# Linear attention beside a delta-rule loop: the query transfers move from SP's queue to GpSimd's

## The chip, the cores and the metric

The kernel runs on one core of a Trainium2 chip. Its time is the device time of one launch in microseconds (us), as the median of several runs. Besides the timed runs one execution was recorded by the hardware profiler; all rows below come from that one. PE is the matrix engine (TensorE; PEld its weight loads), DVE is VectorE, ACT is ScalarE, POOL is GpSimd, and SP is SyncE, which here does nothing but issue DMA transfers. ACT and POOL issue some transfers too. Every engine works through its own instruction list strictly in order: an instruction that waits holds back all that stand behind it on that engine.

## The reference

One layer of a hybrid backbone over 1024 latent tokens and 256 context tokens of width 1024. What is computed, cut to the parts that matter here:

```
h  = modulate(x, norm1_g, sh1, sc1);  hc = modulate(ctx, ...)
zl = h @ w_in;  zc = hc @ w_in                  # three groups of heads
hy  = hyena_mix(zl_hy, ...)                      # long convolutions
gla = gla_branch(zl_gla, zc_gla, ...)            # linear attention, both directions
gdn = gdn_branch(zl_gdn, zc_gdn, ...)            # gated delta rule, both directions
x = x + g1 * (concat([hy, gla, gdn]) @ w_out)
x = x + g2 * (square(relu(modulate(x, norm2_g, ...) @ w1)) @ w2)
out = rmsnorm(x, final_norm_g)

# linear attention, per chunk of 64 tokens
attn = einsum(q, k, exp(b_i - b_j))              # b: running sum of the log gates
o    = (q * exp(b)) @ S + attn @ v
S    = exp(b_last) * S + (k * exp(b_last - b))^T v
```

The delta rule has the same shape of recurrence, one state per head and direction, with a triangular solve inside each chunk.

## The kernel before

The kernel is written with a tile framework that puts the instructions of each engine into one fixed order when the program is built. It works from a timeline of its own, in which each instruction has a priority from its place in the source and a modelled duration; semaphores between the engines are derived from the tiles. So an edit to one line can change the order on every engine.

Stages in time: the Hyena filters, the norm and the input projection; the Hyena convolutions; the preparation and triangular inverses of the delta rule; then, from about 695 to 900 us of the profile, linear attention and the delta-rule loop side by side; then the output projection (`w_out`, line 1706) and the MLP, both as seven-product matrix multiplications in three-pass fp32r (`stage`, line 1518).

Linear attention (`gla_pair`, line 760) works on two pairs of heads, pair 0 and then pair 1. The two heads of a pair lie on partitions 0 to 63 and 64 to 127. For six sizes s = 32 to 1 (levels 0 to 5) DVE and POOL form differences of the running sums, ACT takes their exponential, and DVE multiplies by the queries (line 792) and keys (line 799). The queries `eq` must then lie in a block-diagonal tile `bd`, so that one matmul serves both heads without mixing them: `place` (line 778) copies each half of 64 partitions with a DMA of 256 KB into its own block (line 781). Two `bd` tiles alternate. PE multiplies them with the keys (`pss<-bd,lv`, for the last ones `pss<-bd,kT`), and masked copies collect the result in `A`. Level 6 (the diagonal) is written into `bd` by ACT and has no transfer. Later in the pair, `place` is called once per direction for `q2` (line 882), which PE multiplies with the states `S` (`pss<-S,bd`, line 887). That makes 8 calls a pair, 16 calls and 32 transfers in all. The sources of the transfers are `lv` tiles, four of which rotate; one is free again when its transfer has landed. The pair ends with a norm, transposes (`pss<-ident,A` and `pss<-ident,vt`, line 913), a gate, and stores of its output to DRAM (`dy<-lv`, line 916).

The delta-rule loop (`gdn_head`, line 1122) has ten steps, 0 to 9, for four heads that run abreast. In each step PE multiplies the state with keys and queries (`psl<-S,kq`), solves (`psl<-r,NT`), updates the state (`psl<-vn,kv`) and forms outputs (`psl<-vn,at`). SP loads `at` and `kq` for each step (lines 1135 and 1142), two tiles of each per head; ACT loads `kv`.

After both, `load_y` (line 1343) reads the mixer's outputs back from DRAM into the tiles `h` (`h<-dy`, line 1350; the gates of the delta rule are `h<-dz_dg`, line 1094). These lie in memory that linear attention used. The first products of `w_out` need them, the weights `wr` (from SP, line 1502, and with accumulation from POOL, line 1496), and both split into a high and a low part: ACT casts (`S<-wr`, `T<-h`, line 292), POOL or DVE subtracts (line 252).

Of the kernel before, what the change touches and what calls it, by code (L numbers as in the profile page):

```python
# [17 lines left out]
L = 1024  # L18
# [193 lines left out]
class Build:  # L212
# [547 lines left out]
    def gla_pair(self, p, mid, G):  # L760

        nc = self.nc
# [15 lines left out]
        def place(bd, t):  # L778

            for hh, r in enumerate(halves):  # L780
                nc.sync.dma_start(bd[r, hh].rearrange("p n i -> p (n i)"), t[r, :L])
        for li, s in enumerate((32, 16, 8, 4, 2, 1, 0)):
            bd = self.bd[li % 2]
            if s:
                eq = self.lvt()
                v = lambda t: t[:, :L].rearrange("p (a h s) -> p a h s", h=2, s=s)
                nb = L // (2 * s)
                fm, rm = v(bf)[:, :, 0, s - 1:s], v(rb)[:, :, 1, 0:1]
                self.tt(v(eq)[:, :, 0, :], v(rb)[:, :, 0, :], rm.broadcast_to([128, nb, s]), SUB, self.eng("eqf", 7 * p + li))
                self.tt(v(eq)[:, :, 1, :], v(bf)[:, :, 1, :], fm.broadcast_to([128, nb, s]), SUB, self.eng("eqr", 7 * p + li))  # L790
                self.act(eq[:, :L], eq[:, :L], AF.Exp, scale=1.0 / 16)
                self.tt(eq[:, :L], eq[:, :L], qT, MUL, self.eng("qh0", 7 * p + li))
                place(bd, eq)
                if s > 1:
                    ek = self.lvt()
                    self.tt(v(ek)[:, :, 0, :], fm.broadcast_to([128, nb, s]), v(bf)[:, :, 0, :], SUB, self.eng("ekf", 7 * p + li))
                    self.tt(v(ek)[:, :, 1, :], rm.broadcast_to([128, nb, s]), v(rb)[:, :, 1, :], SUB, self.eng("ekr", 7 * p + li))
                    self.act(ek[:, :L], ek[:, :L], AF.Exp, scale=1.0 / 16)
                    self.tt(ek[:, :L], ek[:, :L], kT[:, :L], MUL, self.eng("kk", 7 * p + li))
                keys = ek if s > 1 else kT  # L800
            else:

                for hh, r in enumerate(halves):
                    self.twice(f"qd{hh}", p, bd[r, hh], c64(qT)[r, :, :])

            ps = self.pss.tile([128, 512], F32, name="pss").rearrange("p (h t i) -> p h t i", h=2, i=32)
            for n in range(16):
                for b in range(2):
                    c = 32 * (b if li else 1 - b)
                    r = 64 * (n % 2) + 32 * b  # L810
# [28 lines left out]
        for s0 in (0, 10):  # L839
            for d in range(2):  # L840
# [3 lines left out]
                for i, n in enumerate(ch):  # L844
                    r = slice(64 * (n % 2), 64 * (n % 2) + 64)
# [22 lines left out]
        for par in range(2):  # L868
            for b in range(2):
                r = slice(64 * par + 32 * b, 64 * par + 32 * b + 32)  # L870
# [7 lines left out]
        for d in range(2):  # L878
            e, q2 = self.lvt(), self.bd[1 - d]
            self.act(e[:, :L], cum[d][:, :L], AF.Exp, scale=1.0 / 16)  # L880
            self.tt(e[:, :L], e[:, :L], qT, MUL)
            place(q2, e)
            for t in range(8):
                for hh in range(2):
                    for par, r in enumerate(halves):
                        n = 2 * t + par
                        self.mm(ps[t // 2][r, t % 2, 96 * hh:96 * hh + 96], q2[:, hh, n, :], S[d][:, n, :], False, d == 1 and hh == 1 and t % 2 == 1)
# [920 lines left out]
```

## Time and profile before

| | us |
|---|---|
| median of 3 runs | 1639.69 (1637.02 to 1644.93) |
| profiled execution | 1637.75 |
| its span, first to last instruction | 1636.0 |
| PE busy | 1507.8 (92%) |
| DVE busy | 1211.8 (74%) |
| ACT busy | 803.2 (49%) |
| POOL busy | 642.4 (39%) |

The shares are averages over stages with different limits. In the stretch in which the change lies, 700 to 880 us, PE is busy for 143.19 of 180 us and POOL for 48.15. DMA-issuing instructions don't count as busy; where they are an engine's own work they are in the timeline of that engine.

### The profile page before, as it was taken

How to read it: one execution, taken by the hardware profiler on the slowest of the kernel's cores; microseconds unless marked ns; L12 is line 12 of the kernel's file. 1: busy time of each engine (PE TensorE's matmuls, PEld its weight loads, DVE VectorE, ACT ScalarE, POOL GpSimd, SP SyncE). 2: the span in 40 equal slices, each digit the busy share in tenths (PEclk: the TensorE clock that was granted, in tenths of full speed). 3: DMA queues.
4: the chain of work that ended last, by engine and by line, in shares of the span. 5: the costliest groups of instructions: out<-in, count | busy, mean ns of one | idle time of the engine just before them, and what ended most of it. 6: DMA issues, size and time to landing. Idle time of an engine off the chain costs nothing. (4 is left out here: it accounts for less than half of the span.)

```text
span 1636.0 us, 26277 instructions
## 1 busy us (share of the span) xinstructions
PE 1507.8 (92%) x10160; PEld 1216.2 (74%) x10160; DVE 1211.8 (74%) x1827; ACT 803.2 (49%) x1462; POOL 642.4 (39%) x478
## 2 busy tenths in 40 slices
PE   7799999989999898768879799999999999999996
PEld 2378877767688676657779587788888888888886
DVE  5963589897575487676678878987679758974995
ACT  5432222315655644454556356554565456446554
POOL 0311141331434330131243254655556555655554
PEclk9999999999999997778889899999999999999998
DMA  8432777756566531267657934364455535453532
GB/s 296 135 110 91 259 256 263 238 180 210 165 205 197 165 134 46 75 192 209 182 148 226 309 103 104 103 155 129 104 132 124 149 87 153 103 136 96 135 72 103
DMA packets 116852, 256.81 MB, mean 157 GB/s; under 512 B 29431, under 2 KB 74919, under 8 KB 103800
## 3 DMA queue, kind: packets, MB, share of 16 engines
q1 hardware_dynamic: 88360, 175.42, 32.4%
q0 software_dynamic: 9808, 59.77, 16.4%
q10 hardware_dynamic: 18560, 19.94, 4.0%
q8 instruction: 80, 1.31, 0.3%
q14 instruction: 44, 0.36, 0.1%
HBM read 196.57 MB, written 41.75 MB: 146 GB/s over the span
## 5 line engine op out<-in xcount | busy, mean ns | idle before, releaser
L224 PE MATMUL psb<-T,S 128*128 128x512 f32 (+1 forms) x3072 | 693.3, 387 | 9.7 <-ACT T L292 6.0
L224 PEld LDWEIGHTS psb<-T,S 128*128 128x128 f32 x3072 | 571.0, 188 | 130.9 <-ACT T L292 6.8
L252 POOL TENSOR_TENSOR S<-wr,S 128x512 fp32r<-128x512 f32 x252 | 365.4, 1465 | 303.2 <-ACT S L292 302.6
L292 ACT CAST S<-wr 128x512 fp32r<-128x512 f32 x252 | 155.1, 620 | 150.0 <-PE psb L224 104.6
L224 PE MATMUL psb<-ahi,wh 128*128 128x512 f32 x448 | 184.5, 413 | 9.3 <-DVE acc L260 4.8
L224 PE MATMUL psb<-alo,wh 128*128 128x512 f32 x448 | 182.8, 408 | 0.0
L224 PE MATMUL psb<-ahi,wl 128*128 128x512 f32 x448 | 181.6, 405 | 0.0
L252 POOL TENSOR_TENSOR wl<-ws,wh 128x1024 fp32r<-128x1024 f32 x28 | 71.1, 2538 | 209.7 <-ACT wh L292 139.1
L260 DVE SCALAR_TENSOR_TENSOR acc<-psb,vecs,acc 128x504 f32<-128x504 f32 (+5 forms) x168 | 111.3, 678 | 49.8 <-ACT acc L264 47.5
L260 DVE SCALAR_TENSOR_TENSOR x<-psb,modT,x 128x512 f32<-128x512 f32 (+1 forms) x148 | 105.2, 727 | 40.2 <-PE psb L224 39.9
L252 DVE TENSOR_TENSOR T<-h,T 128x512 fp32r<-128x512 f32 x88 | 85.8, 1004 | 48.8 <-ACT T L292 47.3
L224 PEld LDWEIGHTS psb<-ahi,wh 128*128 128x128 f32 x448 | 87.8, 196 | 40.7 <-issue 9.1
L252 DVE TENSOR_TENSOR T<-ar,T 128x512 fp32r<-128x512 f32 x112 | 111.0, 1018 | 6.1 <-ACT T L292 5.9
L224 PEld LDWEIGHTS psb<-alo,wh 128*128 128x128 f32 x448 | 87.7, 196 | 26.1 <-issue 8.2
L224 PEld LDWEIGHTS psb<-ahi,wl 128*128 128x128 f32 x448 | 87.6, 196 | 22.5 <-issue 5.1
L292 ACT CAST T<-ar 128x512 fp32r<-128x512 f32 x112 | 68.5, 620 | 44.7 <-DVE ar L260 27.8
L252 POOL TENSOR_TENSOR lv<-cum 128x512 f32<-128x512 f32 x21 | 31.3, 1510 | 83.2 <-PE pss L224 36.9
L264 ACT ACTIVATE acc<-psb,vecs 128x512 f32<-128x512 f32 (+1 forms) x48 | 31.1, 663 | 64.1 <-PE psb L224 31.4
L292 ACT CAST T<-h 128x512 fp32r<-128x512 f32 x88 | 52.6, 619 | 19.5 <-DMA h<-dy 10.4
L264 ACT ACT_TABLE_LOAD x27 | 34.6, 1283 | 35.4 <-DVE acc L260 16.3
L1779 ACT COPY ar<-psb 128x512 f32<-128x512 f32 x48 | 28.2, 587 | 48.2 <-PE psb L224 47.6
L292 ACT CAST wh<-ws 128x1024 fp32r<-128x1024 f32 x28 | 29.3, 1045 | 44.8 <-PE psb L224 35.5
(332 smaller groups left out, 2597.7 us busy)
## 6 DMA issues: line engine op xcount, KB each, us to landing
wr<-in_w SPq DMA_DIRECT2D x40, 1024.0 KB, 4.8
wr<-in_w POOLq DMA_DIRECT2D x24, 1024.0 KB, 8.0
mw<-in_wmod SPq DMA_DIRECT2D x32, 512.0 KB, 5.1
ws<-in_win SPq DMA_DIRECT2D x28, 512.0 KB, 4.1
dft<-in_fw POOLq DMA_DIRECT2D x8, 1024.0 KB, 6.0
dft<-in_iv POOLq DMA_DIRECT2D x8, 1024.0 KB, 6.6
bd<-lv SPq DMA_DIRECT2D x32, 256.0 KB, 4.0
wr<-wr POOLq DMA_DIRECT2D x8, 1024.0 KB, 7.2
```

Of the source, the lines that this page charges most:

```text
L224: return self.nc.tensor.matmul(out, lhsT=lhsT, rhs=rhs, start=start, stop=stop, skip_group_check=more)
L252: return (eng or self.nc.vector).tensor_tensor(out, a, b, op)
L260: return (eng or self.nc.vector).scalar_tensor_tensor(out, a, s, b, op0=op0, op1=op1)
L264: return self.nc.scalar.activation(out, a, f, bias=bias, scale=scale)
L292: self.nc.scalar.copy(hi, src)
L1779: nc.scalar.copy(b[at[i]], ps)
```

## The change

The two DMA instructions of `place` are issued by GpSimd (POOL) instead of SP. Nothing else is edited.

```diff
         def place(bd, t):
 
             for hh, r in enumerate(halves):
-                nc.sync.dma_start(bd[r, hh].rearrange("p n i -> p (n i)"), t[r, :L])
+                nc.gpsimd.dma_start(bd[r, hh].rearrange("p n i -> p (n i)"), t[r, :L])
```

SP's list loses the 32 transfers, POOL's gains them, and the framework puts the work of all engines from about 695 to 945 us into another order. In the rows below a name ends in the number of its tile; `x2` means twice in a row.

On POOL, at the levels of pair 0 (`lv<-cum` forms differences for the keys; its shape is 128 x blocks x s, so 64x8 is level 2, 128x4 level 3, 256x2 level 4), the difference of the two orders is:

```order
 L252 TENSOR_TENSOR lv<-cum 128x16x32
 L252 TENSOR_TENSOR lv<-cum 128x32x16
+L781 DMA bd_6287<-lv 64x1024 x2
+L781 DMA bd_6288<-lv 64x1024 x2
 L252 TENSOR_TENSOR lv<-cum 128x64x8 x2
+L781 DMA bd_6287<-lv 64x1024 x2
 L252 TENSOR_TENSOR lv<-cum 128x128x4 x2
-L252 TENSOR_TENSOR lv<-cum 128x256x2 x2
+L781 DMA bd_6288<-lv 64x1024 x2
+L252 TENSOR_TENSOR lv<-cum 128x256x2
+L781 DMA bd_6287<-lv 64x1024 x2
+L252 TENSOR_TENSOR lv<-cum 128x256x2
```

The transfers of each level now stand between POOL's own instructions for the next levels, and hold them back while they wait.

On PE, at the last products of pair 1 with the states (`pss<-S,bd`), the order before was (tiles vn_8543 to 8549 belong to step 7 of the delta-rule loop):

```order
L224 MATMUL pss<-S_7253,bd_6288 64x96 x16
L224 MATMUL pss<-S_7254,bd_6287 64x96 x24
L224 MATMUL psl<-vn_8545,kv 96x96 x2
L224 MATMUL psl<-vn_8547,kv 96x96 x2
L224 MATMUL psl<-vn_8549,kv 96x96 x2
L224 MATMUL psl<-vn_8543,at_8458 128x96 x2
```

and is now (vn_8704 to 8710 belong to step 8):

```order
L224 MATMUL psl<-vn_8704,at_8619 128x96
L224 MATMUL pss<-vt,lv 64x96 x16
L224 MATMUL pss<-S_7253,bd_6288 64x96 x16
L224 MATMUL pss<-S_7254,bd_6287 64x96 x24
L224 MATMUL psl<-vn_8706,at_8631 128x96 x2
L224 MATMUL psl<-vn_8708,at_8643 128x96 x2
```

These products moved back by about one step of the loop. The transposes behind them (`pss<-ident,A`) moved from behind `psl<-r_8622` of step 8 to behind `psl<-r_8819` of step 9, the last.

On ACT, at the end of the loop, the casts of the first weights of the output projection (`S<-wr_8938`) stood here before, among step 8 and step 9 of the loop:

```order
L237 COPY vn_8708<-psl 128x192
L237 COPY vn_8710<-psl 128x192
L292 CAST S<-wr_8938 128x512 x4
L264 ACTIVATE gsq<-on 128x768
L264 ACTIVATE qs_8833<-psl,cols 128x96 x2
```

and stand now behind all of the loop (vn_8871 is of step 9):

```order
L237 COPY vn_8871<-psl 128x192
L264 ACTIVATE gsq<-on 128x768
L265 ACTIVATE gss<-gss,cst_197 128x8
L292 CAST S<-wr_8938 128x512 x4
L292 CAST T_8943<-h_7615 128x512
```

The accumulating weight transfers of POOL (`wr<-in_wout`) stand behind POOL's work on these casts in both orders, so they moved with them.

## Rows read from the trace of the kernel before

**Rows 1.** Busy time of stretches: PE, PEld, DVE, ACT, POOL, then clock, DMA, GB/s

```profile
700.00:880.00 180.00, 143.19 (x2411) 132.34 (x2408) 127.83 (x271) 95.00 (x222) 48.15 (x43) 0.86 0.65 177
901.00:914.60 13.60, 4.11 (x18) 2.38 (x18) 7.59 (x19) 1.81 (x4) 0.00 (x0) 0.69 1.03 257
920.00:940.00 20.00, 19.15 (x85) 15.51 (x83) 19.85 (x28) 9.00 (x16) 7.49 (x6) 1.00 0.97 334
```

**Rows 2.** Timeline of PE, 862 to 945: start, duration, instruction, [idle before it, releaser]

```profile
875.14 3.52 PE L224 MATMUL pss<-S,bd 128*64 128x96 f32 x80
...
885.77 1.10 PE L287 MATMUL pss<-ident,A 128*128 128x128 f32 x8
...
914.61 24.55 PE L224 MATMUL psb<-T,S 128*128 128x512 f32 x96 [3.42 <-ACT T L292]
```

**Rows 3.** Timeline of SP's transfers at the end of linear attention

```profile
889.13 1.64 SPq L916 DMA_DIRECT2D dy<-lv  x2
894.63 1.66 SPq L1094 DMA_DIRECT2D h<-dz_dg  x3
896.38 17.87 SPq L1350 DMA_DIRECT2D h<-dy  x9
```

**Rows 4.** Timeline of ACT, same place

```profile
913.94 2.78 ACT L292 CAST T<-h 128x512 fp32r<-128x512 f32 x5 [10.08 <-DMA h<-dy]
```

**Rows 5.** Busy time of PE, matmuls into psl (the loop's) alone, 878.66 to 891.67

```profile
878.66:891.67 13.01, 9.83 (x92) 1.00 0.76 257
```

**Rows 6.** Issuing instructions by line: ns min/median/max, first and last start

```profile
L781 SPq DMA_DIRECT2D bd<-lv x32: 462/498/1835, 704.1 to 862.9; - x32
L523 POOL DMA_DIRECT2D fwl<-in_fw x4: 713/720/737, 2.3 to 147.1; - x4
L1496 POOL DMA_DIRECT2D wr<-in_wout x4: 879/887/926, 896.1 to 956.4; - x4
```

**Rows 7.** Transfers of the whole span: count, KB each, median us to landing

```profile
wr<-in_w SPq DMA_DIRECT2D x40, 1024.0 KB, 4.8
wr<-in_w POOLq DMA_DIRECT2D x24, 1024.0 KB, 8.0
...
ws<-in_win SPq DMA_DIRECT2D x28, 512.0 KB, 4.1
...
bd<-lv SPq DMA_DIRECT2D x32, 256.0 KB, 4.0
...
fwl<-in_fw POOLq DMA_DIRECT2D x4, 512.0 KB, 6.1
...
h<-dy SPq DMA_DIRECT2D x8, 256.0 KB, 17.6
```

**Rows 8.** Waits from 695 to 945: us in total, times, longest

```profile
PE pss L224 <- DMA bd<-lv: 14.2, 5, 6.4
```

**Rows 9.** Level 5 of pair 0: DVE's product, then the transfer on SP

```profile
738.09 1.22 DVE L252 TENSOR_TENSOR lv<-lv,qT 128x1024 f32<-128x1024 f32 x1
```

**Rows 10.** Timeline of SP, same place

```profile
742.17 1.11 SPq L781 DMA_DIRECT2D bd<-lv  x2
```

**Rows 11.** Timeline of PE, waits in the middle of the stretch

```profile
746.68 3.21 PE L224 MATMUL pss<-bd,kT 128*32 128x64 f32 x128 [2.59 <-DMA bd<-lv]
...
770.14 2.02 PE L224 MATMUL psl<-S,kq 96*128 96x96 f32 x8 [3.18 <-ACT qs L264]
...
824.43 1.94 PE L224 MATMUL pss<-bd,lv 128*32 128x64 f32 x64 [2.90 <-POOL lv L252]
...
841.32 3.58 PE L224 MATMUL pss<-bd,kT 128*32 128x64 f32 x128 [2.06 <-DMA bd<-lv]
```

**Rows 12.** What SP's queue waited for, 690 to 945: us in total, times, longest

```profile
SPq L1135 <- PE psl L224: 26.0, 10, 9.9
...
SPq L781 <- DVE lv L252: 13.6, 3, 8.7
```

**Rows 13.** The query product on DVE: busy us, mean ns of one, idle before

```profile
L252 DVE TENSOR_TENSOR lv<-lv,qT 128x1024 f32<-128x1024 f32 x16 | 22.7, 1421 | 6.8 <-ACT lv L264 6.8
```

## The prediction

> **What bounds the kernel now.** I read the busy shares first, then the chain of waits, and then, since that chain is not followed back as far as this stretch, the timelines of PE, SP and ACT ahead of it by hand. The change lies in the stretch from 695 to 900 us. There PE leads, but it doesn't fill the time: from 700 to 880 us it is busy for 143.19 of 180 us [rows 1], so some 37 us are waits of a list that is worked through strictly in order. POOL is busy for 48.15 us of the 180 and has room.
>
> What counts is how this stretch hands over to the output projection. The reader should follow one strand: the last products of linear attention with its states end at 875.14 + 3.52 = 878.66; its transposes start at 885.77 [rows 2]; the stores of its output are issued from 889.13 to 890.77; then SP loads the gates, and from 896.38 on nine loads `h<-dy`, the last at about 914 [rows 3]. ACT casts the first of them at 913.94, after 10.08 us of idle time that a load ended [rows 4], and PE begins `w_out` at 914.61 [rows 2]. From 901 to 914.6 PE works for 4.11 of 13.6 us while the DMA engines are full (share 1.03) [rows 1]. So the end of linear attention sets the start of `w_out`, 914.61 - 878.66 = 36.0 us later. The delta-rule loop ends inside those 36 us and is not what ends last.
>
> **The change part by part.** I sum against the profiled execution, 1637.75 us; the median of the runs is 1.94 us above it.
>
> First, the order. On PE the last products of linear attention stand now behind one more step of the loop. What was moved ahead of them is, by the orders, just what PE did in the old run from 878.66 to 891.67: updates and outputs of step 7, the state products, solves and updates of step 8. The loop's matmuls in that window take 9.83 us [rows 5]. All else equal the end of linear attention comes 9.8 us later. Behind it, the transposes wait for the rest of step 8's outputs and step 9's products and solves; that too took about 7 us, the same as from 878.66 to 885.77 before, so the 36.0 us stay as they are. The loop gains what linear attention loses, but its end isn't awaited. Term: +9.8 us. Bounds: 0, if the waits ahead shrink by as much, and +13.0, the window's whole length.
>
> Second, the transfers themselves: 32 of 256 KB, in 16 pairs. The trace has none of this size from POOL. Issue: SP takes 0.498 us for one, POOL 0.720 for one of 512 KB and 0.887 for one of 1 MB [rows 6]; taking 0.72, a pair costs 2 x 0.22 = 0.44 us more. Landing: 512 KB takes 4.1 us from SP and 6.1 from POOL, 1 MB takes 4.8 and 8.0 [rows 7]: POOL's are 2.0 to 3.2 us later. I take 2.0, the nearer size, which makes 2.4 us for a pair with its issue, and keep 0 and 3.6 as ends. Most pairs have cover: PE does the loop's work meanwhile. PE waited five times for these transfers, 14.2 us in all, the longest 6.4 [rows 8]; three of the five are at the first levels of pair 0, where the PE order is nearly unchanged, so there the delay shows in full: 3 x 2.4 = +7.2 us. The ends are 0 and 16 x 3.6 = 58 us, the latter if no pair had cover. The Trainium skill's page "DMA: Bandwidth & Descriptors", in its section on latency, puts the first byte at about 0.6 us for transfers from SP or ACT and at about 1 us for those from GpSimd; by that a pair would be only 0.4 us late and this term 1.2 us. The rows of 512 KB and 1 MB disagree with so small a difference here, so I keep 7.2.
>
> Third, what SP's queue no longer holds back. The level-5 queries of pair 0 were ready on DVE at 738.09 + 1.22 = 739.3 [rows 9], but SP, busy with loads for the loop, issued their transfer at 742.17 [rows 10], and PE idled 2.59 us for it at 746.68 [rows 11]. That goes. Later waits of the same kind are 3.18 us at 770.14, where the loop stood behind a load in SP's queue, and 2.90 and 2.06 us at 824.43 and 841.32, on levels that the new order places a step later, with more of the loop ahead of them [rows 11]. Sum -10.7 us. Bounds: 0, if each turns into another wait, and -18, half of the 37 us of idle PE. SP itself waited 26.0 us for buffers of the loop with transfers of linear attention queued behind, and 13.6 us at the transfers with the loop's loads queued behind [rows 12]; both couplings go. In their place POOL's list couples `place` with POOL's own key differences: a transfer that waits for the queries or a free `bd` holds back the next level's keys. POOL has room, so I cost that at nothing; if the cover fails, it shows as rival A.
>
> Fourth, the loads at the end. Before, the nine `h<-dy` loads (2.25 MB at 256 KB each) shared full DMA engines with two accumulating weight transfers of 1 MB from POOL, the first issued at 896.1 [rows 6], and took 17.6 us each to land [rows 7]. Now those weight transfers stand behind casts that follow the whole loop on ACT, so they start several us into the loads. Without them the same bytes would need 2.25/4.25 of the time: up to 8 us less. I take -3, since they still come before the loads are done. If the weights arrive late, the second product of `w_out` would wait instead; the first covers them with half of the 24.55 us of rows 2, some 12 us.
>
> Sum: 9.8 + 7.2 - 10.7 - 3 = +3.3 us; 1637.75 + 3.3 + 1.94 = 1643.0 us. After 915 us the orders are almost the same and I expect a rigid shift.
>
> **The rivals.** A, slower: POOL's list becomes the thing that linear attention waits for. Its transfers wait for DVE's products and for free `bd` tiles, its key differences wait behind them, and PE, in order, waits with the loop's work queued behind. Place: the levels of both pairs. It decides as soon as the delay shows at eight or more of the 16 pairs instead of three. At eight: 9.8 + 8 x 2.4 - 10.7 - 3 = +15.3, so 1655 us. For it: the five waits of rows 8 show that PE's list has little slack at the levels. Against: the new order puts more of the loop between the levels of pair 1.
>
> B, faster: the loop and linear attention really come apart. The loads of the loop are always early, PE's idle 37 us shrink by half, 18 us, the loads at the end gain 3, and the delay of the transfers stays hidden: 9.8 - 18 - 3 = -11, so 1629 us. For it: rows 12. Against: linear attention now ends last by order, and everything at the end hangs on it.
>
> C, a lock: POOL's issuing is held up by DVE. If each of the 32 issues waited for half of a DVE instruction of 1.421 us [rows 13], 23 us would come on top of the sum, were all of it exposed: 1666 us. Against it stand POOL's four issues of 1 MB around 896 to 956 us, which took 0.879 to 0.926 us, hardly spread [rows 6], although DVE was busy for 19.85 of 20 us there [rows 1]. The Trainium skill's page "SBUF — State Buffer" (the warning on DVE blocking DMA) says that GpSimd cannot write its descriptors while DVE runs an operation in a two-port mode, such as an fp32 copy within SBUF, and advises issuing from SP or ACT; by that rule C could happen. The narrow spread of those four issues does not bear it out for this mix of DVE work.
>
> D: nothing moves. The delay of the transfers and the order cancel against the idle time: 1639.7 us.
>
> **How the numbers follow.** Less than about 0.5% (8.2 us) can't be told from no change. The forecast, 1643 with a spread of some 8 us around it, has 0.35; D 0.1; A 0.3; C 0.05; B 0.2. The forecast and D lie within 0.5% (1631.5 to 1647.9), A and C above, B below: faster 0.2, same 0.45, slower 0.35. The range leaves out C, the far end of A and the far end of B: 1626 to 1660 us; the forecast's own range is 1635 to 1651.
>
> **What would show it.** The order term: the last `pss<-S,bd` should end near 885 to 892 us, and PE's `w_out` start near 918 (914.6 + 3.3), with the transposes of linear attention behind the last solves of the loop. The transfer term: landings of `bd<-lv` near 6 us instead of 4.0, and longer PE waits for them at the first three levels of pair 0. The SP term: few waits of the loop for `at` or `kq`. The loads: `h<-dy` landing in less than 17.6 us. I am wrong if `w_out` starts before 908 (B), if PE's waits for `bd<-lv` sum to well over 25 us (A), if POOL's issues spread far above 0.9 us (C), or if the shift at 915 us isn't found again at the end.

## The result

The changed kernel takes 1655.1 us in the median against 1638.4 us for the kernel before: ratio 1.0104, 95% interval 1.0066 to 1.0141, some 17 us slower. Run again, beside other kernels, it was 1652.7 against 1641.7 us, ratio 1.0063 (1.0036 to 1.0089). So it is slower by 0.6 to 1.0%; the forecast was 1643.0 us, no measurable change. Below, "before" is the kernel before, "after" the changed one; rows of before are named by their group.

The profiled execution of after took 1650.32 us, its span 1648.5 us. Timeline of PE, after, the rows that answer to [rows 2]:

```profile
888.33 3.52 PE L224 MATMUL pss<-S,bd 128*64 128x96 f32 x80
...
900.62 1.04 PE L287 MATMUL pss<-ident,A 128*128 128x128 f32 x8
...
920.12 8.58 PE L224 MATMUL psb<-T,S 128*128 128x512 f32 x29
929.76 0.51 PE L224 MATMUL psb<-T,S 128*128 128x512 f32 x1 [1.06 <-ACT T L292]
...
936.86 1.64 PE L224 MATMUL psb<-T,S 128*128 128x512 f32 x4 [1.99 <-ACT S L292]
940.52 10.26 PE L224 MATMUL psb<-T,S 128*128 128x512 f32 x36 [2.02 <-POOL S L252]
...
955.50 46.70 PE L224 MATMUL psb<-T,S 128*128 128x512 f32 x204 [1.68 <-ACT T L292]
```

The last products with the states end at 888.33 + 3.52 = 891.85 instead of 878.66: 13.2 us later. `w_out` starts 5.5 us later (920.12 against 914.61), but then it halts several times, while before its first 96 matmuls ran through in 24.55 us. The long run of 204 matmuls that follows starts at 955.50; in before it is this row of the same view:

```profile
941.72 46.72 PE L224 MATMUL psb<-T,S 128*128 128x512 f32 x204 [2.57 <-ACT T L292]
```

That is +13.8 us, close to the 13.2 us at the end of linear attention. A late start is not the whole hand-over: the first products need only the first loads. SP's transfers of after, answering to [rows 3], say why:

```profile
902.69 0.32 SPq L916 DMA_DIRECT2D dy<-lv  x1
...
904.42 7.27 SPq L1094 DMA_DIRECT2D h<-dz_dg  x3
911.74 5.78 SPq L1350 DMA_DIRECT2D h<-dy  x9
```

The first `h<-dy` is issued at 911.74 instead of 896.38. Those that come last are waited for inside `w_out`.

The transfers themselves, by line (ns min/median/max, first and last start) and from issue to landing (us min/median/max), after and then before:

```profile
L781 POOL DMA_DIRECT2D bd<-lv x32: 510/525/600, 707.5 to 878.2; - x32
DMA to landing us min/median/max: 2.9/4.5/8.3
```

```profile
DMA to landing us min/median/max: 3.2/4.0/5.9
```

An issue takes POOL 0.525 us, hardly more than SP's 0.498 [rows 6] and far from the 0.72 that I took; the median landing is 0.5 us later, not 2.0. The two rows of landings aren't over the same transfers, though: the trace has a landing for all 32 of POOL's, but for only 23 of SP's in before. At those 23 places after is 0.3 us later in the median and 7.4 us at most, against 5.9; its 8.3 us fall on a transfer for which before has no landing. PE's waits for them, after, in 695 to 945 (us in total, times, longest), and two of the waits in the timeline of PE:

```profile
PE pss L224 <- DMA bd<-lv: 16.1, 4, 6.3
```

```profile
744.90 1.94 PE L224 MATMUL pss<-bd,lv 128*32 128x64 f32 x64 [4.76 <-DMA bd<-lv]
...
814.80 1.94 PE L224 MATMUL pss<-bd,lv 128*32 128x64 f32 x64 [1.25 <-DMA bd<-lv]
```

The total is little above the 14.2 us of [rows 8], only at other places. A list of waits by releaser doesn't show the loss here. The window of [rows 1] does, after:

```profile
700.00:880.00 180.00, 147.18 (x2320) 137.24 (x2316) 132.85 (x277) 100.24 (x234) 64.05 (x79) 0.80 0.67 186
```

PE is busy for 4 us more and the window shows 91 matmuls fewer, at a mean clock of 0.80 instead of 0.86. So PE's time has to be split. I cut the stretch from the first product with `bd` (711.95 after, 708.68 before) to the last `pss<-S,bd` into pieces of 2.5 us and added up, from PE busy and granted clock of each: idle time; busy time times (1 - clock), the time lost to the lower clock; and the rest, the work at full clock (5.00 us busy at a clock of 0.50 count as 2.5 us of work and 2.5 lost). "To the restart" is from that end to the run of 204 matmuls For all kernels, in us of one profiled execution each:

| kernel | ratio (95%) | stretch | work | idle | lower clock | to the restart |
|---|---|---|---|---|---|---|
| before | 1 | 170.0 | 117.7 | 30.4 | 21.8 | 63.1 |
| after | 1.0104 (1.0066-1.0141) | 179.9 | 126.2 | 25.4 | 28.2 | 63.7 |
| pool_again (after) | 1.0063 (1.0036-1.0089) | 178.2 | 127.1 | 31.6 | 19.5 | 63.7 |
| sp_in_new_order | 1.0052 (1.0027-1.0077) | 174.3 | 126.6 | 25.6 | 22.1 | 63.9 |
| pool_in_old_order | 1.0114 (1.0077-1.0151) | 183.7 | 115.0 | 38.9 | 29.8 | 61.6 |
| act_issues | 0.9977 (0.9949-1.0006) | 164.7 | 114.6 | 25.7 | 24.4 | 62.4 |
| act_in_old_order | 1.0014 (0.9988-1.0041) | 169.6 | 117.1 | 31.1 | 21.4 | 61.1 |
| sp_in_act_order | 1.0000 (0.9973-1.0027) | 159.3 | 116.0 | 23.2 | 20.1 | 64.7 |
| pool_old_vt_later | 1.0135 (1.0110-1.0161) | 184.0 | 114.6 | 36.1 | 33.3 | 62.6 |
| pool_pair0 | 1.0067 (1.0041-1.0093) | 178.3 | 122.7 | 32.6 | 23.0 | 60.3 |
| pool_pair1 | 1.0051 (1.0022-1.0080) | 180.2 | 129.1 | 27.6 | 23.5 | 59.4 |
| pool_old_dve_keys | 1.0101 (1.0071-1.0130) | 183.9 | 115.2 | 35.8 | 32.9 | 61.9 |
| sp_old_dve_keys | 0.9983 (0.9962-1.0003) | 163.3 | 116.6 | 25.8 | 20.9 | 61.5 |
| sp_old_four | 1.0054 (1.0033-1.0076) | 174.4 | 116.7 | 31.2 | 26.5 | 62.8 |

The last column moves by 5.3 us (59.4 to 64.7) while the end itself moves over 27 us: the end of linear attention sets the rest, whatever `w_out` does at its start. In after the stretch holds 8.5 us more work: the delta-rule step that the new order puts ahead of its end. Single executions of one kernel differ by several us, so the ratios decide and the columns explain. The work column itself is good to about 3 us: the kernels in the order of before, whose PE does the same in this stretch, show 114.6 to 117.7.

### The profile page after: what moved, and what is told of

Read it like the earlier page. It is cut to its first block, busy times and chain, and to the rows that moved or that the text cites. A ratio compares the mean times of both kernels' runs of the same rounds, so it can differ in the third digit from the quotient of the medians.

```text
span 1648.5 us, 26314 instructions
## 1 busy us (share of the span) xinstructions
PE 1519.3 (92%) x10160; PEld 1225.0 (74%) x10160; DVE 1219.3 (74%) x1827; ACT 805.3 (49%) x1464; POOL 658.2 (40%) x510
## 5 line engine op out<-in xcount | busy, mean ns | idle before, releaser
L252 DVE TENSOR_TENSOR T<-h,T 128x512 fp32r<-128x512 f32 x88 | 92.4, 1075 | 53.0 <-ACT T L292 51.7
L224 PEld LDWEIGHTS psb<-alo,wh 128*128 128x128 f32 x448 | 87.9, 196 | 25.7 <-issue 7.8
L264 ACT ACTIVATE acc<-psb,vecs 128x512 f32<-128x512 f32 (+1 forms) x48 | 31.1, 662 | 62.5 <-PE psb L224 29.8
L264 ACT ACT_TABLE_LOAD x28 | 35.9, 1283 | 36.1 <-DVE acc L260 17.2
L1779 ACT COPY ar<-psb 128x512 f32<-128x512 f32 x48 | 28.2, 587 | 48.2 <-PE psb L224 47.6
L260 DVE SCALAR_TENSOR_TENSOR ar<-ar 128x512 f32<-128x512 f32 x32 | 45.6, 1445 | 0.0
```

Source lines behind the costliest of these rows:

```text
L224: return self.nc.tensor.matmul(out, lhsT=lhsT, rhs=rhs, start=start, stop=stop, skip_group_check=more)
L252: return (eng or self.nc.vector).tensor_tensor(out, a, b, op)
L260: return (eng or self.nc.vector).scalar_tensor_tensor(out, a, s, b, op0=op0, op1=op1)
L264: return self.nc.scalar.activation(out, a, f, bias=bias, scale=scale)
L1779: nc.scalar.copy(b[at[i]], ps)
```

## The experiments

To separate the issuer from the order, a kernel is built twice: first with one issuer, to take each engine's order from it, then with another, where every instruction but the 32 transfers is tied to follow its predecessor in that order (a tie without a semaphore). The tie holds the order, but not the buffers: which of the four `lv` buffers a tile gets stays the framework's choice, and in the program of pool_in_old_order 15 of the 49 `lv` tiles lie in another buffer than in that of before (16 in act_in_old_order, 28 between pool_old_dve_keys and its control sp_old_dve_keys). Below, one such choice matters.

```diff
+    _, order = build(PLAN)        # the order of each engine under one issuer
+    nc, _ = build(ISSUER, order)  # the transfers issued by another
+                for n in order:
+                    if n in b.placed: continue      # the 32 transfers stay free
+                    if e in last: tc.add_manual_dep(i, last[e], dep, reason="order")
```

**pool_in_old_order** (issuer POOL, order of before).

> POOL issues the query transfers, as after the change, but the instructions of every engine stand in the order of the kernel before (only the 32 transfers themselves move, from SP's list to POOL's). Theory T1, the order costs the time: this kernel has the time of before, ratio 0.997 to 1.003 (within 5 us), with the last products with the states ending near 879 us. Theory T2, POOL as the issuing engine costs it (later transfers, a list in which they hold back the key differences): 8 to 17 us slower than before, ratio 1.005 to 1.010, with PE's waits for the transfers above 16 us.

**sp_in_new_order** (issuer SP, order of after).

> SP issues the transfers, as before the change, but the instructions of every engine stand in the order of the changed kernel. T1, the order: as slow as the changed kernel, ratio 1.007 to 1.012 (11 to 19 us above before), last products with the states ending near 889 us or later. T2, the issuing engine: the time of before, ratio 0.997 to 1.003.

**pool_again** (after, unchanged) and **act_issues** (`nc.scalar.dma_start` in `place`, order left to the framework).

> The changed kernel once more, on the same chip as its two halves. Both theories: ratio 1.007 to 1.013, 11 to 21 us above before.

> ACT issues the transfers, which gives a third order: by it the last products of linear attention with the states stand ahead of the outputs of step 7 of the loop, as in the kernel before. T1: the time follows that place, so ratio 0.996 to 1.003. T2: what counts is that an engine with work of its own issues (here the one whose exponentials feed the levels), so ratio 1.005 to 1.012. A third outcome, faster than before by 0.5% or more, would need that SP's held-up loads (26.0 us of waits) really cost time on PE.

Measured: 1.0114, 1.0052, 1.0063, 0.9977. T1 as I stated it falls at the first of them: with no change of order POOL as the issuer costs 18.7 us. T2 falls at the second: with SP as the issuer the new order costs 8.5 us. 1.0052 and 1.0063 lie below the ranges that T1 gave (1.007 and up), and 1.0114 lies above that of T2. Both cost, and they don't add up: under the new order POOL and SP are 0.0011 apart, within their intervals (by the first measurement of after, 1.0104, they would be 0.0052 apart). Where the transfers come late, the extra step of the loop is work that PE has while it waits; this reading of why they don't add up is argued, not tested. ACT as the issuer costs nothing.

Where the 18.7 us arise is seen in pool_in_old_order: idle +8.5 and lower clock +8.0 us against before, at the same work but for the error of the split (-2.7). Its stretch is 13.7 us longer. PE at levels 0, 1 and 5 of pair 1 and at the last products with the states, before and then pool_in_old_order (the rows of before that are missing here are in [rows 2] and [rows 11]):

```profile
807.40 1.10 PE L224 MATMUL pss<-bd,lv 128*32 128x64 f32 x64
...
810.76 1.10 PE L224 MATMUL pss<-bd,lv 128*32 128x64 f32 x64 [0.47 <-DVE lv L260]
```

```profile
809.01 1.10 PE L224 MATMUL pss<-bd,lv 128*32 128x64 f32 x64
...
819.81 1.93 PE L224 MATMUL pss<-bd,lv 128*32 128x64 f32 x64 [6.27 <-DMA bd<-lv]
...
851.07 3.36 PE L224 MATMUL pss<-bd,kT 128*32 128x64 f32 x128 [0.55 <-DMA bd<-lv]
...
892.16 3.52 PE L224 MATMUL pss<-S,bd 128*64 128x96 f32 x80
```

It is 1.6 us behind at level 0, 9.1 at level 1, 9.8 at level 5 and 17.0 at the last products. So nearly all of it is lost at two places: ahead of level 1 and, behind level 5, at the `q2` of pair 1, to which I come below. At level 1 POOL and SP did this:

```profile
807.78 2.56 POOL L252 TENSOR_TENSOR lv<-cum 128x512 f32<-128x512 f32 x2 [6.44 <-DMA bd<-lv]
810.29 0.60 POOL L237 COPY mid<-vt 128x512 f32<-128x512 f32 x1
810.84 1.05 POOL L781 DMA_DIRECT2D bd<-lv  x2
```

```profile
810.91 0.56 SPq L820 DMA_DIRECT2D vt<-dvt  x1
```

DVE had these queries ready at 808.43. POOL was first waiting for an earlier transfer, then forming a difference and copying `mid`; that copy is also the last reader of `vt`, so it releases SP's 960 KB load of the next `vt` in the same instant, and the transfer runs beside it: 9.0 us until PE goes on. Before, SP issued the transfer at 806.15 and the load behind it at 807.68, and PE went on at 810.76:

```profile
806.15 1.11 SPq L781 DMA_DIRECT2D bd<-lv  x2
807.68 0.58 SPq L820 DMA_DIRECT2D vt<-dvt  x1
```

The Trainium skill's page "DMA: Bandwidth & Descriptors" (section "SWDGE vs HWDGE vs iDMA") says that GpSimd's transfers and those of SP or ACT have different queues inside each DMA engine, between which it takes turns; that fits the 9 us. But a queue of its own is not enough for them: in act_in_old_order the pair is on ACT's queue, issued at 806.41, 1.2 us ahead of the load, and PE goes on 5.1 us after the issue. Being issued in the same instant as the load and being on another queue than the load are not told apart by any run.

**pool_old_vt_later** moves that load (its expectation calls the transfer level 0's; counted as in the code it is level 1's):

```diff
+    MOVES = [(['I-7252'], 'I-8459')]   # SP: vt<-dvt ahead of at<-dAT of step 7
```

> POOL issues the transfers in the old order, as in pool_in_old_order, and one load is moved: SP issues the 960 KB load of pair 1's values (vt, line 820) some 25 us later, still ahead of its use. Theory T3, collision: in pool_in_old_order the level-0 transfer of pair 1, issued on POOL's queue at 810.84, ran beside that load (SP, 810.91) and PE waited 6.27 us for it; in the kernel before both were on SP's queue, the transfer first. Without the collision that wait falls below 2.5 us, the last products with the states end 4 to 6 us earlier, and the ratio falls from 1.0114 to 1.007 to 1.009. Rival, POOL's list alone: the transfer was issued 2.4 us after DVE had its queries ready, because POOL was busy; then the wait stays above 4 us and the ratio at 1.010 to 1.013.

Measured: 1.0135, not better than 1.0114. The load is now issued 17.3 us later. PE, then SP, then POOL:

```profile
815.05 1.10 PE L224 MATMUL pss<-bd,lv 128*32 128x64 f32 x64 [1.66 <-DVE lv L252]
...
838.32 1.94 PE L224 MATMUL pss<-bd,lv 128*32 128x64 f32 x64 [7.28 <-DMA bd<-lv]
```

```profile
828.24 0.56 SPq L820 DMA_DIRECT2D vt<-dvt  x1
```

```profile
828.57 1.08 POOL L781 DMA_DIRECT2D bd<-lv  x2
```

Level 1 now lands in time (issued at 810.70, PE on at 815.05), so the sign of the rival, a wait above 4 us there, is gone; but the load has met the transfer of level 3, for which PE waits until 9.8 us after its issue. The collision was moved, not removed, so what it costs in all stays open: this run neither shows T3 as an account of the time nor refutes it.

**act_in_old_order** (`build("scalar", order)`, order of before).

> ACT issues the transfers, every engine in the old order. If what cost 18 us in pool_in_old_order is POOL itself (its slower landing, 4.6 against 4.0 us in the median, and its list of key differences), this kernel has the time of before, ratio 0.997 to 1.003. If it is that the transfers left SP's queue, where they stood ahead of the big loads, ratio 1.006 to 1.012, with a wait of PE of 4 us or more for level 0 or 1 of pair 1.

Measured: 1.0014. It is POOL, not the leaving of SP's queue: ACT's list is as closely tied to the levels, and its transfers land in 4.0 us in the median, as SP's do. The slower landing that the expectation lays to POOL is hardly there: at the 23 places where before has a landing, pool_in_old_order is 0.3 us later in the median. Its slowest, 10.4 us, is the second `q2` of pair 0, for which before has none; from ACT the same transfer took 10.2 us.

**pool_pair0** and **pool_pair1** split the change by pair:

```diff
-                nc.sync.dma_start(bd[r, hh]...
+                (nc.sync, nc.gpsimd)[p == 0].dma_start(bd[r, hh]...   # pool_pair1: p == 1
```

> POOL issues the transfers of pair 0 only, SP those of pair 1; the framework orders anew. In the profile of the changed kernel pair 0 was 9 us late at level 5 and in time again at its end, while pair 1 lost all of the 13 us. Theory: only pair 1's transfers cost, so ratio 0.999 to 1.004. Rival, the exposed first levels of pair 0 are the cost: 1.005 to 1.010. By the new order the last products with the states stand ahead of the updates of step 8, half a step later than before, which by itself would be about 5 us, 1.003.

> POOL issues the transfers of pair 1 only, SP those of pair 0; the framework orders anew, and the last products with the states stand behind the updates of step 8, as in the changed kernel. Theory (the cost arises in pair 1): ratio 1.005 to 1.011. Rival (it arises in pair 0): 0.998 to 1.003.

Measured: 1.0067 and 1.0051. Either half alone costs about as much as the whole did in pool_again, and 1.0067 is outside the range of the theory that only pair 1 costs. But both have new orders with 5 and 11 us more work in the stretch, so this doesn't tell order from transfers.

**pool_old_dve_keys** and its control **sp_old_dve_keys** (order of before) take the work on the levels out of POOL's list:

```diff
+    def keys(self, key, i): return self.nc.vector if self.ondve else self.eng(key, i)
-                self.tt(v(ek)[:, :, 0, :], ..., SUB, self.eng("ekf", 7 * p + li))
+                self.tt(v(ek)[:, :, 0, :], ..., SUB, self.keys("ekf", 7 * p + li))   # and eqf, eqr, ekr, kk
```

> POOL issues the transfers in the old order, and all work of POOL on the levels (the differences of queries and keys and one product with the keys) is put on DVE, at the same places of the order, so that nothing of the levels stands between POOL's transfers. Theory L, the list: in pool_in_old_order POOL waited for a transfer to land before it formed the next key difference, and the next transfer stood behind that; without this the kernel is within 5 us of sp_old_dve_keys (ratios less than 0.003 apart). Theory Q, the queue: POOL's transfers land later whatever stands in its list (4.6 against 4.0 us in the median, tails of 10 us); then it is at least 8 us slower than sp_old_dve_keys (0.005 or more), ratio about 1.010.

> The control of pool_old_dve_keys: the same work moved from POOL to DVE, old order, SP issues. DVE has the room for most of it (0.65 us for a difference that takes POOL 1.25), so ratio 0.997 to 1.006 by both theories.

Measured: 1.0101 against 0.9983, some 19 us apart: the differences and the product in POOL's list are not what costs, so theory L as worded falls. Theory Q doesn't follow from it. At the 22 places where the control has a landing, POOL's are 0.05 us later in the median. And the copies `mid` and `A2` were left on POOL, so the transfers behind them (level 1 of pair 1, the first `q2` of pair 1) aren't cleared of the list: they are issued 1.55 and 1.65 us after DVE had the queries ready. The difference arises there and at one more place, the first `q2` of pair 0: PE is 1.3 us behind the control at level 5 of pair 0, 8.9 at the end of pair 0, 15.1 at level 1 of pair 1, 14.2 at level 5 and 19.9 at the last products. First the `q2` of pair 0. In the control, SP, ACT and PE:

```profile
760.54 1.11 SPq L781 DMA_DIRECT2D bd<-lv  x2
```

```profile
765.54 1.06 ACT L264 ACTIVATE lv<-cum 128x1024 f32<-128x1024 f32 x1 [1.80 <-DMA bd<-lv]
```

```profile
768.16 1.13 PE L224 MATMUL psl<-S,kq 96*128 96x96 f32 x8 [0.66 <-ACT qs L264]
...
769.58 1.09 PE L224 MATMUL psl<-S,kq 96*128 96x96 f32 x8
```

and with POOL as the issuer, POOL, ACT and PE:

```profile
762.10 1.02 POOL L781 DMA_DIRECT2D bd<-lv  x2 [2.27 <-DVE sc L260]
```

```profile
768.31 1.06 ACT L264 ACTIVATE lv<-cum 128x1024 f32<-128x1024 f32 x1 [3.27 <-PE pss L224]
```

```profile
766.75 1.43 PE L224 MATMUL pss<-vt,lv 64*64 64x96 f32 x36
...
770.93 1.13 PE L224 MATMUL psl<-S,kq 96*128 96x96 f32 x8 [2.13 <-ACT qs L264]
...
772.65 1.91 PE L224 MATMUL psl<-S,kq 96*128 96x96 f32 x8
```

POOL's list is free there: DVE's product ended at 761.81 and the issue follows 0.3 us later. ACT's next exponential starts 6.2 us after the issue instead of 5.0, but not because the transfer is late. In the control it waits for the transfer, as its row says. With POOL the two halves land 3.4 and 4.1 us after their own issues, by 766.7, and the exponential starts at 768.31: its row names PE, whose products `pss<-vt,lv` end at 768.18. In the two programs the exponential writes into different `lv` buffers: in the control into the one that the transfer reads, with POOL into the one that these products read. So this place shows the cost of a buffer that the framework chose differently. Behind the exponential on ACT stand the loop's `qs`, so PE idles 2.13 us instead of 0.66, and then its clock falls: the same eight matmuls take 1.91 us instead of 1.09. Windows of that place, control first (PE, PEld, DVE, ACT, POOL busy, then clock, DMA, GB/s):

```profile
775.00:780.00 5.00, 5.00 (x111) 4.64 (x112) 3.02 (x8) 1.19 (x5) 0.00 (x0) 1.00 0.57 121
```

```profile
775.00:780.00 5.00, 5.00 (x44) 4.35 (x43) 1.63 (x7) 1.11 (x4) 0.00 (x0) 0.50 1.01 261
780.00:785.00 5.00, 5.00 (x46) 4.53 (x42) 3.37 (x10) 1.64 (x6) 0.00 (x0) 0.50 0.63 167
```

So a pause that is 1.5 us longer has become 7.6 us (1.3 to 8.9), most of it at the 1.2 GHz level of the clock. It is no part of the 18.7 us against before: there PE idled 3.18 us at the same place [rows 11], with the clock at 0.50 from 770 to 785 behind it.

At the first `q2` of pair 1 it is POOL's list. POOL, then ACT, in pool_in_old_order:

```profile
859.83 5.69 POOL L237 COPY lv<-A 32x512 f32<-32x512 f32 x8
865.60 0.59 POOL L252 TENSOR_TENSOR on<-on,qs 128x192 f32<-128x192 f32 x1
866.13 1.06 POOL L781 DMA_DIRECT2D bd<-lv  x2
```

```profile
870.88 1.06 ACT L264 ACTIVATE lv<-cum 128x1024 f32<-128x1024 f32 x1 [5.61 <-DMA bd<-lv]
```

DVE had these queries ready at 864.48, and the transfer was issued 1.65 us later, behind the eight copies `A2` and an instruction of the loop; before, SP issued it 0.02 us after DVE (854.96 and 854.98). Here ACT's exponential does wait for the transfer. PE idles 2.22 us ahead of 873.51, then works at half clock.

```profile
870.00:875.00 5.00, 2.78 (x26) 2.48 (x27) 3.03 (x10) 3.18 (x9) 1.02 (x2) 0.95 0.76 220
875.00:880.00 5.00, 5.00 (x36) 4.61 (x34) 3.13 (x14) 2.22 (x7) 1.13 (x2) 0.50 0.97 229
880.00:885.00 5.00, 5.00 (x52) 4.78 (x50) 3.40 (x11) 2.35 (x7) 0.64 (x2) 0.50 0.83 268
```

In before the clock is 1.00 throughout 865 to 890. So both places at which pool_in_old_order falls behind are transfers that stand behind POOL's own work in its list, the copies in both cases. That is read from the rows; no run takes these copies off POOL.

**sp_old_four** gives SP's transfers a dose of lateness (order of before):

```diff
+                w = L // 2
+                for c in range(0, L, w):
+                    nc.sync.dma_start(bd[r, hh]...[:, c:c + w], t[r, c:c + w])
```

> SP issues, old order, but each half is transferred in two pieces of 128 KB, so that a pair takes four issues and its last piece is issued about 1.1 us later than before: a dose of lateness without POOL. If a lateness of about 1 us at every level is enough for the loss (theory Q): ratio 1.005 to 1.012. If the loss is the coupling in POOL's list (theory L): 0.998 to 1.003.

Measured: 1.0054 (1.0033 to 1.0076), about 9 us, without POOL: a lateness of about this size is enough for a loss, wherever it comes from, so this doesn't choose between POOL's queue and its list. SP's queue also holds 32 more issues here, so it is no pure dose.

**sp_in_act_order** (order of act_issues, issuer SP).

> SP issues, every engine in the order that the framework makes when ACT issues. act_issues in that order was at 0.998, and ACT in the old order at 1.001. If the order is the better one by itself: 0.994 to 0.999, the fastest so far. If ACT's queue made it (loads of the loop and transfers apart): 1.000 to 1.005.

Measured: 1.0000. That order is no better by itself. No kernel beat before by more than the measurement can tell (best: 0.9977 and 0.9983); both of these beat the changed one.

## Why the forecast was off

**The order, +9.8: right.** The stretch holds 8.5 and 9.4 us more work in the two profiles of that kernel, and sp_in_new_order, where SP still issues, is 8.5 us slower (4 to 13 by its interval). Of the 13.2 us by which the end moved in the first profile, 3.3 were there at the first product already, ahead of the first transfer.

**The transfers, +7.2: wrong in size per transfer, and no term that can be added.** A pair lands 0.3 us later in the median where both landings are known, and its two issues add 0.05 us; I had 2.4 in all. The page "DMA: Bandwidth & Descriptors" of the Trainium skill ("Latency and other measured facts"), with 0.6 and 1 us to the first byte, was nearer than the rows of larger transfers that I preferred. But in the old order POOL as the issuer costs 18.7 us, and in the new one some 2 (by the intervals, between nothing and 8): I priced the order and the lateness each against before, though the one decides how much of the other is covered. And I cost the coupling in POOL's list at nothing because POOL has room on the average; at the two places where pool_in_old_order falls behind, the transfer was issued 2.4 and 1.65 us after DVE had it ready, behind POOL's own work.

**SP's queue, -10.7: this step failed.** The waits named there are gone by name (level 5 of pair 0 no longer waits), but PE idles 25.4 and 31.6 us in the two profiles against 30.4 before, and lost 28.2 and 19.5 us to the lower clock against 21.8. On the average of the two nothing came back. act_in_old_order shows it without a change of order: the transfers leave SP's queue there too, and the kernel takes 1.0014 of the time, with 31.1 us idle. A wait that goes in a list worked through in order lets the next one show, here 4.76 us at level 4. One of the four waits didn't belong in the sum at all: the 2.90 us at 824.43 are given by their row to POOL's product with the keys, not to a transfer [rows 11].

**The loads, -3: nothing.** POOL's accumulating weight transfers did start later (912.65 against 896.12), and `h<-dy` still lands in 16.7 us instead of 17.6 [rows 7]. What `w_out` gained at its start it gave back waiting for `h` and the weights. "A rigid shift after 915" holds from the restart on.

So by these runs the sum should have been 9.8 plus about 2, 1651.5 us against the measured 1652.7 and 1655.1; the 2 is what the runs leave over, not a price worked out from rows. **Rival A** named the time (1655) but not the place: with the new order four waits, not eight, are exposed. Its mechanism shows in the old order, with nine waits and 22.6 us. **Rival C** is out: POOL's issues take 510 to 600 ns, in a stretch where DVE is busy for 132.85 of 180 us; for this mix of DVE work the trace shows nothing of what the warning of the Trainium skill's page "SBUF — State Buffer" (DVE blocking DMA) describes. **B** and **D** are out by the time.

What stays open: how much of the 18.7 us is the place behind `mid` and `A2` in POOL's list, how much the load that meets the transfer of level 1, and how much other buffers and the later landing. No run takes the copies off POOL, and none ties the buffers.

## What to carry to other kernels

Price a new issuer and the new order together: what the order adds as work it may give back as cover. Where PE runs close to its waits, count a longer pause with what follows it, here 1.5 us that became 7.6 through the lower clock. With a framework that orders and places anew, look also at which buffer a tile got: a tied order is not the same program. And judge a hand-over by the point from which the work runs through again, not by its first instruction.

## What the runs showed of the hardware

- POOL issues 256 KB in 0.525 us, 512 KB in 0.720 and 1 MB in 0.887 [rows 6]: the larger ones don't price the smaller (they differ in kind too: the first is within SBUF, the others load from DRAM, the last with accumulation). SP's issue is 0.498 us in before, ACT's 0.48 to 0.51, for 256 KB.
- A transfer issued by POOL within 0.4 us of a 960 KB load from SP was waited for until 9 to 10 us after its issue, at five places (805.79 in after, 805.52 in pool_again, 810.84 in pool_in_old_order, 828.57 in pool_old_vt_later, 809.37 in pool_old_dve_keys). When the transfer was issued first, the load 1.2 to 1.6 us behind it, PE went on 4.6 to 5.1 us after the issue, with both on SP's queue (before, sp_old_dve_keys) and with the transfer on ACT's (act_in_old_order).
- PE after a longer pause: 0.66 us of idle time and the clock stayed at 1.00, 2.13 us at the same place and it was 0.50, the 1.2 GHz level, from 775 to 785 (sp_old_dve_keys and pool_old_dve_keys).
